# A transformer layer on one core: held and separate PSUM banks, 128-row gate sums, and casts issued behind bank copies

## The chip, the cores and the metric

One core of a Trainium2 chip runs the kernel. The metric is the device time in microseconds; the kernel before took 1955.86 us (median of 1954.67, 1955.86 and 1956.07). TensorE (PE) multiplies, VectorE (DVE) and ScalarE (ACT) do elementwise work, GpSimd (POOL) little, and SyncE (SP) issues DMAs.

## What is computed

One layer in f32, with T = 256 tokens, D = 2048 and DFF = 5632: two SwiGLU blocks with a token mixer between them, each modulated by columns of a vector `ada` and closed by a residual and a layer norm.

```python
ada = silu(c) @ w_ada + b_ada                   # 9 x 2048: shift, scale, gate of three blocks
h = swiglu(modulate(x, sh1, sc1), ffn1_w_in, ffn1_w_out)
x = layernorm(ALPHA * x + 0.5 * (1 + g1) * h, ln1_g, ln1_b)
z = modulate(x, sh2, sc2) @ w_in                # mixer
#   fox attention, 8 heads of 128: softmax(q k / sqrt(128) + F[q] - F[k], causal) v,
#     F = cumsum(log_sigmoid(forget gate))
#   mLSTM, 4 heads, 128 wide keys, 256 wide values: gates i and f, a running maximum,
#     rms norm, times sigmoid(o)
x = layernorm(ALPHA * x + (1 + g2) * (concat(fox, mlstm) @ w_out), ln2_g, ln2_b)
h = swiglu(modulate(x, sh3, sc3), ffn2_w_in, ffn2_w_out)
x = layernorm(ALPHA * x + 0.5 * (1 + g3) * h, ln3_g, ln3_b)
```

## The kernel before, in words

**Products.** Each f32 operand is split into a rounded part `hi` and the rest `lo` (both fp32r), and each product is three (`mm3`, L376 to L379: hi·hi, hi·lo, lo·hi). `load_w` (L359) brings a weight piece of 1 MB into one of three `raw` slots by an SP DMA, and `split` makes `hi` with an ACT cast (L145) and `lo` with a DVE subtraction (L146), in two or four parts, into six slots each. Products add up in PSUM banks of 512 f32 columns: five for `mm_tile`, three for `aux_tile`.

**Stages**, by the trace in us: start 0 to 40; first stage to 310; the rest of ffn1's input product (`ffn_in`) to 540; its output product (`out_proj`) to 770; a boundary with residual, layer norm, modulation and transposes to 840; the mixer to 1150, its output product to 1190; the second boundary to 1230; ffn2 to 1650 and 1938; the tail (`to_out`) to 1951.

**First stage** (`first_in`, L751). While the vector `ada` is still being made, the input product of ffn1 runs in four quarters j of the contraction, each with the same twelve units i of 48 products. A unit fills two banks; they are drained into SBUF (`hT`) at the end of each unit, by an ACT copy in quarter 0 and by DVE additions (L767) later. Last comes SiLU, 256 columns at a time. Beside it, `first_ada` makes the modulation columns of the next quarter: DMA'd rows `ar` are multiplied into an accumulator by DVE (L158 first, then L160; one named `gate` in even quarters). Of eight loads per quarter six sit in `raw` slots of the weights. Four pairs of column products (L718) and four small additions (L720) follow, between the four quarters of the modulated x (`xhi_f`, `xlo_f` L319). Later rows of `ada` go through `acc` (L160) throughout the kernel, a few pieces at a time ("pump", "step").

**out_proj** holds back its last weight pieces and does row block a = 0 of the last columns before a = 1 (`last_products`, L438). Where a boundary follows, a = 0's products are made as two passes of 256 columns; `add_up` (L447) multiplies the bank by the gate row (L453), adds the residual (L455) and takes the statistics (L457). The tail does so with both row blocks, scales (L613), shifts (L618) and stores (L619).

**Mixer.** `cols_form_b` and `form_a_pair` make the columns of w_in, ten groups: sigmoid inputs `mo` come ahead of them, then `fv` and `mv` (values), pairs `m` and `f` (queries and keys). Copies by ACT bring the banks to SBUF. Heads are generators in a list `side`, and a `step` after each half group takes a piece of one. A fox head (L985) puts into a bank q·k of two query blocks (128 and 256 keys wide, plain f32) and, for each, twice an 8-row product (L995) that adds the row −F (`nfrow`, hi and lo): a column of `rowsel` spread over 128 columns selects the head's row. An mLSTM head (L1103) does the same with 4-row products for `gb` (L1110). `gates` (L1044) makes those rows. The sigmoids `og` (L1173) read the `mo` banks; `ytp` (L1159) are transposes of mLSTM results; `bc` and L214 make a gate row of ada.

A scheduler of the tile framework orders each engine's instructions, by its own costs; `tc.manual_schedule` keeps an engine in program order, `tc.issue_after(x)` puts what is issued behind x, and an engine executes its list strictly in order. What a DMA or a semaphore wait stops on an engine stops all behind it.

## Time and profile before

| What | Value |
|---|---|
| Time, median of 3 | 1955.86 us (1954.67 to 1956.07) |
| The profiled execution | 1953.24 us, of which the trace spans 1951.1 |
| PE busy | 1898.5 us, 97% |
| DVE, ACT busy | 1461.1 us (75%), 939.9 us (48%) |
| Chain that ended last | PE 92%, DVE 5%, DMA 1% |
| Read from memory | 506.71 MB, 261 GB/s over the span |

A row of the timeline has its start, its duration, engine, line, operation, output tile and inputs, shapes and a count; a bracket holds idle time of the engine just before it and what ended that. A count over 1 groups rows of one form that follow each other, and the duration is then of all. Matmul rows overlap: what one costs PE is the distance from its start to the next one's, not its length. A plain f32 product appears as two records.

### The profile page before, as it was taken

What the parts mean: (1) busy time and instruction counts of PE and PEld (TensorE: products, weight loads), DVE (VectorE), ACT (ScalarE), POOL (GpSimd) and SP (SyncE); (2) the same over time, 40 slices, a digit from 0 to 9 for tenths busy, and PEclk for the clock granted to TensorE, in tenths of its full rate; (3) what the DMA queues carried; (4) which work ended last, traced back from release to release, by engine and by line L of the source; (5) the groups of instructions that cost most, each with busy time, mean ns of one, the idle gap of its engine ahead of it and who ended that gap; (6) DMA issues with size and microseconds to landing.
All of it is one profiled execution on the core that took longest, in us unless ns stands there. A gap on an engine that the chain in (4) does not pass through costs nothing.

```text
span 1951.1 us, 32572 instructions
## 1 busy us (share of the span) xinstructions
PE 1898.5 (97%) x13297; PEld 1741.2 (89%) x13297; DVE 1461.1 (75%) x1773; ACT 939.9 (48%) x1306; POOL 19.0 (1%) x34
## 2 busy tenths in 40 slices
PE   3999999999999999999999999999999999999997
PEld 3999999999988888598998886999999999988886
DVE  7889889777778898678877677767776654555776
ACT  2654454444444554645754544555444444444552
POOL 0000000000000000000000000000000000000000
PEclk9999999999999999999999999999999999999999
DMA  8999869999889887589878784997777755655552
GB/s 325 347 334 332 304 211 318 326 307 328 293 304 317 272 296 234 163 299 320 294 245 290 246 263 150 321 311 263 238 268 257 231 193 193 233 187 190 194 194 87
DMA packets 301821, 510.92 MB, mean 262 GB/s; under 512 B 10818, under 2 KB 158690, under 8 KB 300648
## 3 DMA queue, kind: packets, MB, share of 16 engines
q1 hardware_dynamic: 300808, 505.70, 76.5%
q0 software_dynamic: 864, 3.15, 0.5%
q8 instruction: 104, 1.70, 0.4%
q14 instruction: 45, 0.37, 0.1%
HBM read 506.71 MB, written 2.10 MB: 261 GB/s over the span
## 4 chain that ended last, share of the span: by engine, by line
PE 92%; DVE 5%; DMA 1%; issue 1%; ACT 1%; POOL 0%; DVEq 0%; SPq 0%; POOLq 0%; ACTq 0%
PE gu_f L379 8%; PE gu_f L377 8%; PE gu_f L378 8%; PE o_f L377 8%; PE o_f L379 8%; PE o_f L378 8%; PE s L377 5%; PE s L379 5%; PE s L378 5%; PE pr_f L378 2%; PE pr_f L377 2%; PE pr_f L379 2%; PE fh L377 2%; PE fh L378 1%; PE fh L379 1%; PE fs L378 1%
## 5 line engine op out<-in xcount | busy, mean ns | idle before, releaser
L160 DVE SCALAR_TENSOR_TENSOR acc<-ar,csil,acc 128x1024 f32<-128x1024 f32 x242 | 307.0, 1269 | 24.6 <-DMA ar<-in_w_ada_dram 23.8
L377 PE MATMUL s<-xhi_f,hi_s 128*128 128x256 f32 x768 | 213.5, 278 | 0.6 <-ACT hi_s L145 0.6
L378 PE MATMUL s<-xlo_f,hi_s 128*128 128x256 f32 x768 | 213.2, 278 | 0.0
L379 PE MATMUL s<-xhi_f,lo_s 128*128 128x256 f32 x768 | 212.9, 278 | 0.0
L379 PE MATMUL gu_f<-xhi_f,lo_f2i 128*128 128x256 f32 x768 | 212.0, 276 | 0.0
L378 PE MATMUL gu_f<-xlo_f,hi_f2i 128*128 128x256 f32 x768 | 212.0, 276 | 0.0
L377 PE MATMUL gu_f<-xhi_f,hi_f2i 128*128 128x256 f32 x768 | 212.0, 276 | 0.0
L146 DVE TENSOR_TENSOR lo_f2i<-raw_f2i,hi_f2i 128x1024 fp32r<-128x1024 f32 x96 | 117.6, 1225 | 99.9 <-ACT hi_f2i L145 99.8
L377 PE MATMUL gu_f<-xhi_f,hi_f1i 128*128 128x256 f32 x640 | 176.8, 276 | 0.0
L379 PE MATMUL gu_f<-xhi_f,lo_f1i 128*128 128x256 f32 x640 | 176.7, 276 | 0.0
L378 PE MATMUL gu_f<-xlo_f,hi_f1i 128*128 128x256 f32 x640 | 176.7, 276 | 0.0
L145 ACT CAST hi_f2i<-raw_f2i 128x1024 fp32r<-128x1024 f32 x96 | 100.8, 1050 | 137.5 <-PE gu_f L378 125.5
L145 ACT CAST hi_s<-raw_s 128x1024 fp32r<-128x1024 f32 x96 | 97.3, 1049 | 102.7 <-DMA raw_s<-in_ffn_w_in_dram 58.9
L377 PEld LDWEIGHTS s<-xhi_f,hi_s 128*128 128x128 f32 x768 | 145.2, 189 | 0.7 <-ACT hi_s L145 0.7
L145 ACT CAST hh<-hT 128x512 fp32r<-128x512 f32 x128 | 78.6, 621 | 138.6 <-PE o_f L378 136.9
L378 PEld LDWEIGHTS s<-xlo_f,hi_s 128*128 128x128 f32 x768 | 145.2, 189 | 0.0
L379 PEld LDWEIGHTS s<-xhi_f,lo_s 128*128 128x128 f32 x768 | 144.8, 189 | 0.3 <-DVE lo_s L146 0.3
L378 PEld LDWEIGHTS gu_f<-xlo_f,hi_f2i 128*128 128x128 f32 x768 | 144.2, 188 | 0.1
L377 PEld LDWEIGHTS gu_f<-xhi_f,hi_f2i 128*128 128x128 f32 x768 | 144.1, 188 | 0.1
L379 PEld LDWEIGHTS gu_f<-xhi_f,lo_f2i 128*128 128x128 f32 x768 | 144.2, 188 | 0.0
L146 DVE TENSOR_TENSOR lo_f2o<-raw_f2o,hi_f2o 128x1024 fp32r<-128x1024 f32 x88 | 107.7, 1224 | 44.9 <-ACT hi_f2o L145 44.8
L377 PE MATMUL o_f<-hi_f2o,hh 128*128 128x512 f32 (+1 forms) x368 | 139.4, 379 | 0.0
(451 smaller groups left out, 5357.6 us busy)
## 6 DMA issues: line engine op xcount, KB each, us to landing
ar<-in_w_ada_dram SPq DMA_DIRECT2D x288, 512.0 KB, 5.8
raw_s<-in_ffn_w_in_dram SPq DMA_DIRECT2D x48, 1024.0 KB, 5.9
raw_f2i<-in_ffn_w_in_dram SPq DMA_DIRECT2D x48, 1024.0 KB, 5.1
raw_f1o<-in_ffn_w_out_dram SPq DMA_DIRECT2D x44, 1024.0 KB, 7.2
raw_f2o<-in_ffn_w_out_dram SPq DMA_DIRECT2D x44, 1024.0 KB, 5.1
raw_f1i<-in_ffn_w_in_dram SPq DMA_DIRECT2D x40, 1024.0 KB, 7.8
raw_mxo<-in_w_out_dram SPq DMA_DIRECT2D x16, 1024.0 KB, 7.3
raw_fh<-in_ffn_w_in_dram SPq DMA_DIRECT2D x16, 1024.0 KB, 7.6
```

Of the source, the lines that this page charges most:

```text
L145: S.copy(hi, src)
L146: V.tensor_tensor(out=lo, in0=src, in1=hi.bitcast(F32), op=ALU.subtract)
L160: ins = V.scalar_tensor_tensor(out=acc, in0=raw, scalar=csil[:, k:k + 1], in1=acc, op0=ALU.mult, op1=ALU.add)
L377: PE.matmul(o, ah, bh, start=start, stop=False)
L378: PE.matmul(o, ah, bl, start=False, stop=False)
L379: return PE.matmul(o, al, bh, start=False, stop=stop)
```

## The change

1. *Ends by a bank of their own* (`last_products`, `add_up`): the last products of a row block run 512 wide up to the last four k; for those, columns 0 to 255 are finished in the old bank and columns 256 to 511 in a second bank `oh`. The first bank is multiplied by the gate row and added over all 512 columns, then `oh` is over its 256. In the tail both row blocks end so; at both boundaries too, where a = 1 was one pass of 512 columns. The tail's shifts and stores are put in another order, two pieces of 256 last for each row block.
2. *Held banks*: quarter j + 1 starts with the unit with which quarter j ended (`order_of`), so that unit goes on in the same two banks and is not drained between. SiLU is done 512 wide when both its parts are there. From the second quarter on, all eight column products go into one bank with one addition. The sums of the next quarter's `ada` are issued behind the last `xlo` of the current one (`behind`).
3. *128-row products*: −F's hi and lo stand in rows 0 to 7 and 32 to 39 of one tile `frows` of 128 rows, the rest zero, with the first 128 keys repeated, so that one product of 384 columns adds all of a fox head's rows; likewise `grows` for an mLSTM head.
4. *Casts behind bank copies*: in a group of the mixer, the splits of all weight pieces but the first are issued behind the last copy out of the previous group's banks (`emptied`). The sigmoids count as such copies, and a one-column sigmoid (`table`) is issued ahead to load the table.

```diff
     def load_w(src, nk, w, name, place=None, copies=()):
...
-            split(raw[:, q * h:(q + 1) * h, :], hi, lo)
+            with behind_copies(copies):
+                split(raw[:, q * h:(q + 1) * h, :], hi, lo)
...
+            def last_products(a):
+                half[a, 0] = mm_tile(f"oh_{tag}{a}")
+                args = held[:-kn] + (kept if a else []) + held[-kn:]
+                body, end = args[:-4], args[-4:]
+                with tc.issue_after(last[0].ins) if a else nullcontext():
+                    products(a, body, k0, None)
+                    products(a, end, None, ends[1], w=256)
+                    last.append(products(a, end, *ends, outs=half, c=256, w=256))
...
             def add_up(a, ps=ps, col=col, bs=range(nb), half=half):
...
+                    cs = slice(c0, c0 + 512)
+                    V.tensor_tensor(out=p, in0=p, in1=gate[:, cs], op=ALU.mult)
+                    V.scalar_tensor_tensor(out=r, in0=r, scalar=ALPHA, in1=p, op0=ALU.mult, op1=ALU.add)
+                    if half:
+                        p, cs = half[a, b][:, 256:], slice(c0 + 256, c0 + 512)
+                        V.tensor_tensor(out=p, in0=p, in1=gate[:, cs], op=ALU.mult)
+                        V.tensor_tensor(out=res[:, a, cs], in0=res[:, a, cs], in1=p, op=ALU.add)
...
     def to_out(products, add_up, st, lgb):
...
-                if a:
-                    second(0, 1536, 2048)
-                    second(1, 0, 256)
-                    second(1, 256, 512)
-                for j in range(a, 3 + a):
+                for j in range(3):
                     second(a, j * 512, (j + 1) * 512)
+                for j in range(2):
+                    second(a, 1536 + j * 256, 1792 + j * 256)
...
     def first_ada(j, ws=iter(())):
...
+            with behind(modulated[0]):
+                for h in range(2):
...
+        if j:
+            columns()
...
     def first_in(j, n, i, ws):
+        old = held.pop(i, None)
+        pss = old or [mm_tile(f"s{j}_{i}_{b}") for b in range(2)]
+        hold = n == NS - 1 and j < 3
+        if hold:
+            held[i] = pss
+            return
+    def order_of(j):
+        return [i % NS for i in range(NS - j, 2 * NS - j)]
...
     def fox_head(qs, h):
+        PE.matmul(lps[:, :3 * P], row_of(h), frows, start=True, stop=False)
         for qt in range(2):
-            PE.matmul(lps[:, cs], qs[:, 0, qt * P:(qt + 1) * P], qs[:, 1, :nk], start=True, stop=False)
-            for i in range(2):
-                PE.matmul(lps[:, cs], rowsel[:, h:h + 1].to_broadcast([8, P]), nfrow[i][:, :nk],
-                          start=False, stop=i == 1)
+            PE.matmul(lps[:, cs], qs[:, 0, qt * P:(qt + 1) * P], qs[:, 1, :P * (qt + 1)],
+                      start=False, stop=qt == 1)
...
-        for i in range(2):
-            PE.matmul(gb[:, :T], rowsel[:4, h:h + 1].to_broadcast([4, P]), ng[i], start=i == 0, stop=i == 1)
+        PE.matmul(gb[:, :T], row_of(h), grows, start=True, stop=True)
...
+    table = sm.tile([P, 1], F32, tag="table", bufs=1, name="table")
+    tc.keep_in_program_order(S.activation(table, ident[:, 0:1], AF.Sigmoid))
     for a in range(2):
         for h in range(NMH):
-            S.activation(og[h][:, a, :MV], mps[a, h // 2][:, h % 2 * MV:(h % 2 + 1) * MV], AF.Sigmoid)
+            sig = S.activation(og[h][:, a, :MV], mps[a, h // 2][:, h % 2 * MV:(h % 2 + 1) * MV], AF.Sigmoid)
+    emptied.append(sig)
```

On PE, where the pair group f0 ends, before (`ytp` are mLSTM transposes, `lps` a fox head's scores, `pr_f` the next group):

```order
L379 MATMUL pr_f_10672<-xhi_mx,lo_f0b_10923 128x256
L1159 MATMUL ytp_10958<-ident,og_8634 128x128 x4
L1159 MATMUL ytp_10969<-ident,og_8635 128x128 x4
L993 MATMUL lps_10980<-qs_10353 128x128
L995 MATMUL lps_10980<-nfrow_8644,rowsel 128x128
L995 MATMUL lps_10980<-nfrow_8645,rowsel 128x128
L993 MATMUL lps_10980<-qs_10353 128x256
L995 MATMUL lps_10980<-nfrow_8644,rowsel 128x256
L995 MATMUL lps_10980<-nfrow_8645,rowsel 128x256
L377 MATMUL pr_f_11024<-xhi_mx,hi_f1a_11028 128x256
```

The same place with the change (lines are those of the changed kernel):

```order
L390 MATMUL pr_f_10595<-xhi_mx,lo_f0b_10846 128x256
L1220 MATMUL ytp_10881<-ident,og_8554 128x128 x4
L1220 MATMUL ytp_10892<-ident,og_8555 128x128 x4
L1051 MATMUL lps_10903<-frows,rowsel 128x384
L1054 MATMUL lps_10903<-qs_10277 128x128
L1054 MATMUL lps_10903<-qs_10277 128x256
L388 MATMUL pr_f_10941<-xhi_mx,hi_f1a_10945 128x256
```

Four products of a head with 8 rows have become one with 128, ahead of the two of q and k.

On ACT, at the start of the mixer, before (`hi_fv` are casts of the value weights, `og` the sigmoids of the `mo` banks):

```order
L351 CAST xhi_mx<-xf_8427 128x2x128
L145 CAST hi_fv_00_8675<-raw_fv_0_8673 128x520
L145 CAST hi_fv_01_8691<-raw_fv_0_8673 128x520
L145 CAST hi_fv_02_8707<-raw_fv_0_8673 128x520
L145 CAST hi_fv_03_8723<-raw_fv_0_8673 128x520
L145 CAST hi_fv_10_8745<-raw_fv_1_8743 128x520
L1173 ACT_TABLE_LOAD
L1173 ACTIVATE og_8632<-mo_8436 128x256
L1173 ACTIVATE og_8633<-mo_8436 128x256
L1173 ACTIVATE og_8634<-mo_8437 128x256
L1173 ACTIVATE og_8635<-mo_8437 128x256
```

And with the change:

```order
L356 CAST xhi_mx<-xf_8347 128x2x128
L1233 ACT_TABLE_LOAD
L1233 ACTIVATE table<-ident 128x1
L145 CAST hi_fv_00_8599<-raw_fv_0_8597 128x520
L145 CAST hi_fv_01_8615<-raw_fv_0_8597 128x520
L145 CAST hi_fv_02_8631<-raw_fv_0_8597 128x520
L145 CAST hi_fv_03_8647<-raw_fv_0_8597 128x520
L1236 ACTIVATE og_8552<-mo_8356 128x256
L1236 ACTIVATE og_8553<-mo_8356 128x256
L1236 ACTIVATE og_8554<-mo_8357 128x256
```

The table load and a small sigmoid stand four casts ahead of the sigmoids, and the cast of fv's second weight piece (`hi_fv_10`) has moved behind them.

On DVE, at the end of the first quarter of the first stage, before (`lo_s` weights, `gate<-ar` the sums of ada, `scsh` the modulation columns, `xlo_f` the next quarter's x):

```order
L146 TENSOR_TENSOR lo_s_00_1068<-raw_s_0_1065,hi_s_00_1067 128x1024
L146 TENSOR_TENSOR lo_s_01_1072<-raw_s_0_1065,hi_s_01_1071 128x1024
L158 TENSOR_SCALAR gate<-ar_2_0_1075,csil 128x1024
L720 TENSOR_TENSOR scsh<-cp_987,bcol 128x2
L720 TENSOR_TENSOR scsh<-cq_988,bcol 128x2
L160 SCALAR_TENSOR_TENSOR gate<-ar_2_0_1075,csil,gate 128x1024
L720 TENSOR_TENSOR scsh<-cp_987,bcol 128x2
L720 TENSOR_TENSOR scsh<-cq_988,bcol 128x2
L319 TENSOR_TENSOR xlo_f_121<-xf_653,xhi_f_120 128x256 x4
L146 TENSOR_TENSOR lo_s_10_1135<-raw_s_1_1132,hi_s_10_1134 128x1024
L146 TENSOR_TENSOR lo_s_11_1139<-raw_s_1_1132,hi_s_11_1138 128x1024
L160 SCALAR_TENSOR_TENSOR gate<-ar_2_1_1142,csil,gate 128x1024 x2
```

And with the change:

```order
L146 TENSOR_TENSOR lo_s_110_1062<-raw_s_11_1059,hi_s_110_1061 128x1024
L146 TENSOR_TENSOR lo_s_111_1066<-raw_s_11_1059,hi_s_111_1065 128x1024
L739 TENSOR_TENSOR scsh<-cp_987,bcol 128x2x4
L324 TENSOR_TENSOR xlo_f_121<-xf_653,xhi_f_120 128x256 x4
L158 TENSOR_SCALAR gate<-ar_2_0_1069,csil 128x1024
L146 TENSOR_TENSOR lo_s_00_1127<-raw_s_0_1124,hi_s_00_1126 128x1024
L160 SCALAR_TENSOR_TENSOR gate<-ar_2_0_1069,csil,gate 128x1024
L146 TENSOR_TENSOR lo_s_01_1131<-raw_s_0_1124,hi_s_01_1130 128x1024
L160 SCALAR_TENSOR_TENSOR gate<-ar_2_1_1134,csil,gate 128x1024 x2
L146 TENSOR_TENSOR lo_s_10_1194<-raw_s_1_1191,hi_s_10_1193 128x1024
L146 TENSOR_TENSOR lo_s_11_1198<-raw_s_1_1191,hi_s_11_1197 128x1024
```

The four additions of columns are one, the four `xlo_f` come ahead of the sums, and a weight's `lo` stands between the sums of the first load.

More of the change, by code (lines that the diff above doesn't have):

```diff
@@ L438, in last_products @@
[L438 to L447 removed]
+                for k, hh, hl, hi, lo in args:
+                    for b in range(nb):
+                        bs = slice(b * 512 + c, b * 512 + c + w)
+                        mm = mm3(outs[a, b][:, c:c + w], hh[:, ts_], hl[:, ts_], hi[:, bs], lo[:, bs],
+                                 k == k0, k == k1)
@@ L712, in first_ada, with columns @@
             yield
-        cps = aux_tile(f"cp{j}"), mm_tile(f"cq{j}")
+        cps = aux_tile(f"cp{j}"), mm_tile(f"cq{j}") if j == 0 else None
+        def columns():
+            for q in range(4):
+                for v in range(2):
+                    PE.matmul(cps[0][:, 4 * v + q:4 * v + q + 1], acc[:, v, q * P:(q + 1) * P], ones[:, 0:1],
+                              start=True, stop=True)
+            js = slice(4 * j, 4 * j + 4)
+            V.tensor_tensor(out=scsh[:, 0:2, js], in0=cps[0][:, :8].rearrange("p (v k) -> p v k", v=2),
+                            in1=bcol[:, 0:2, js], op=ALU.add)
+        if j:
+            columns()
+            for _ in mb:
+                pass
+            yield
+            return
         def column(q):
@@ L978, in layer_kernel, with row_of @@
     fcol, mcol = ccol[:, :, 0:8], ccol[:, :, 8:12]
-    nfrow = [mx.tile([8, T], F32R, name=f"nfrow{i}") for i in range(2)]
-    rowsel = mx.tile([8, 8], F32R, name="rowsel")
-    V.tensor_copy(rowsel, ident[:8, :8])
+    frows = mx.tile([P, 3 * P], F32R, name="frows")
+    grows = mx.tile([P, T], F32R, name="grows")
+    lg2 = mx.tile([P, 2, 40], F32, name="lg2")
+    for t in (frows.bitcast(F32), grows.bitcast(F32), lg2):
+        G_.memset(t, 0.0)
+    rowsel = mx.tile([P, 8], F32R, name="rowsel")
+    V.tensor_tensor(out=rowsel, in0=ident[:, 0:8], in1=ident[:, 32:40], op=ALU.add)
+    def row_of(h):
+        return rowsel[:, h:h + 1].to_broadcast([P, P])
     def fox_head(qs, h):
```

141 lines of the change are left out of this document (73 added, 68 removed).

## The prediction

> **What bounds the kernel now.** I read the page's busy times first, then the table by stage, then PE's waits, then the timeline at each place that the diff touches.
>
> ```profile
> PE 1898.5 (97%) x13297; PEld 1741.2 (89%) x13297; DVE 1461.1 (75%) x1773; ACT 939.9 (48%) x1306; POOL 19.0 (1%) x34
> ```
>
> PE is busy for all but 53 us. By stage (PE, PEld, DVE, ACT and POOL busy, clock, DMA share, GB/s):
>
> ```profile
> 0.00:40.00 40.00, 7.49 (x32) 6.67 (x33) 29.09 (x43) 7.43 (x12) 2.37 (x11) 1.00 0.94 343
> 125.00:148.00 23.00, 23.00 (x205) 23.00 (x205) 22.19 (x24) 7.99 (x8) 0.00 (x0) 1.00 0.93 331
> 171.00:194.00 23.00, 23.00 (x202) 22.82 (x202) 22.78 (x31) 11.31 (x17) 0.73 (x1) 1.00 0.97 325
> 540.00:750.00 210.00, 210.00 (x944) 173.03 (x943) 179.89 (x194) 108.34 (x133) 0.53 (x1) 1.00 0.86 295
> ...
> 840.00:1150.00 310.00, 307.61 (x2135) 282.44 (x2135) 233.90 (x343) 174.25 (x297) 1.65 (x1) 1.00 0.83 281
> 1935.00:1952.00 17.00, 3.44 (x29) 3.24 (x27) 10.88 (x19) 0.00 (x0) 1.52 (x1) 0.69 0.34 123
> ```
>
> PE idles for 32.5 us at the start, which the change leaves alone, and for 13.6 us at the end, where DVE and the output's DMAs run; elsewhere for under 8 us. So what shortens PE's own stream in the mixer (840:1150) shortens the kernel, if loads keep up. The pace is 23/205 = 0.112 us for a 256-wide product and 210/944 = 0.222 for a mostly 512-wide one. In the first stage PE never stops, but DVE has only 0.8 and 0.2 of 23 us to spare in two of the stretches: that stage has nothing to give and something to lose. PE's waits between start and end are few; the two longest have their rows in parts 2 and 3, the next is that of the two boundaries (us in total, times, longest):
>
> ```profile
> PE tp L335 <- ACT n L331: 1.0, 2, 0.5
> ```
>
> **The change, part by part.** 1. *Rows of 128 in the mixer.* A fox head's scores, eight times in the program, and an mLSTM head's, four times:
>
> ```profile
> 1041.10 0.39 PE L993 MATMUL lps<-qs 128*128 128x128 f32 x2
> 1041.41 0.43 PE L995 MATMUL lps<-nfrow,rowsel 8*128 8x128 f32 x2
> 1041.78 0.70 PE L993 MATMUL lps<-qs 128*128 128x256 f32 x2
> 1042.40 0.50 PE L995 MATMUL lps<-nfrow,rowsel 8*128 8x256 f32 x2
> 1042.83 0.39 PE L377 MATMUL pr_f<-xhi_mx,hi_f1a 128*128 128x256 f32 x1
> 1043.05 0.28 PE L378 MATMUL pr_f<-xlo_mx,hi_f1a 128*128 128x256 f32 x1
> ...
> 952.93 0.28 PE L379 MATMUL pr_m<-xhi_mx,lo_m1b 128*128 128x256 f32 x1
> 953.14 0.50 PE L1110 MATMUL gb<-ng,rowsel 4*128 4x256 f32 x2
> 953.57 0.70 PE L1112 MATMUL sps<-o 128*128 128x256 f32 x2
> ```
>
> From start to start a fox head holds PE for 1042.83 − 1041.10 = 1.73 us, and the next product is 0.1 late: 1.83. The two kinds of product alternate. The 8-row ones take 0.37 + 0.43 = 0.80, the f32 ones 0.31 + 0.62 = 0.93, a change of kind included in each. Afterwards one 384-wide product of 128 rows, at 0.222 × 384/512 = 0.17, stands ahead of both f32 ones. With 0.93 for those the head takes 1.10 and saves 0.73; without the changes of kind between 128-row products (about 0.1 each, by the gap of 0.21 ahead of gb against 0.11) up to 1.0. I take 0.91: **−7.3** for eight (−5.8 to −8.0). For gb two products of 0.43 together become one of 0.11: 0.32, and 0.2 more if both changes of kind go; I take 0.32, **−1.3** for four (to −2.1). If 128 rows cost per column what 8 rows cost, half the columns go from lps (0.40) and half from gb (0.21): 8 × 0.50 + 4 × 0.21 = −4.9 in all, the small end.
>
> The Trainium skill, "TensorEngine Tiling (Array Packing)", section "Overview", speaks against this edit: a contraction of 32 rows or fewer leaves the array mostly unused and should be packed in tiles, up to four at once, not padded. No tiles run together here, and the rows show 0.2 us for 256 columns of 8 rows against 0.11 for 128 rows. Its section "Tiling Modes" says that a change of mode drains the engine; the 0.1 us ahead of gb agrees.
>
> 2. *Sigmoids (og) of the mixer.* The sigmoids' table load, and ahead of it a cast that waited 4.27 us for a slot, stand between the mo products and their banks:
>
> ```profile
> 836.64 0.63 ACT L145 CAST hi_fv<-raw_fv 128x520 fp32r<-128x520 f32 x1 [4.27 <-PE mo L379]
> 837.29 1.28 ACT L1173 ACT_TABLE_LOAD   x1
> 838.59 1.77 ACT L1173 ACTIVATE og<-mo 128x256 f32<-128x256 f32 x6
> 839.30 0.39 PE L377 MATMUL b_fv<-hi_fv,xhi_mx 128*128 128x264 f32 x1 [1.69 <-ACT og L1173]
> ```
>
> Afterwards the load goes four casts ahead and that cast behind the eight sigmoids. ACT idled 4.27 us, so 1.28 is covered there, and the first bank's sigmoids can run as its products end. PE gets back 1.69 + 0.2 around it: **−1.9** (0 if the sigmoids still come late). Behind the last sigmoid now wait the casts of fv's second load; the first load's four, split before, give PE 48 products, 5.4 us, meanwhile.
>
> 3. *A gate behind an ada sum.*
>
> ```profile
> 1025.09 0.40 PE L180 MATMUL bc<-alo,trir 128*128 128x512 f32 x1
> 1025.24 1.28 DVE L160 SCALAR_TENSOR_TENSOR acc<-ar,csil,acc 128x1024 f32<-128x1024 f32 x1 [3.59 <-DMA ar<-in_w_ada_dram]
> ...
> 1027.58 1.28 DVE L214 SCALAR_TENSOR_TENSOR gate<-bc,gate 128x512 f32<-128x512 f32 x2
> 1028.32 0.66 PE L1159 MATMUL ytp<-ident,og 128*128 128x128 f32 x4 [2.39 <-DVE gate L214]
> ```
>
> DVE stood for 3.59 us at a sum whose rows had not landed; the gate, and PE behind it, waited. In the new order that sum follows both gates. They can start when bc ends, at about 1025.5, so PE's wait goes: **−2.4** (0 if the lo now ahead is late instead). Next late is the sum itself, which nobody awaits.
>
> 4. *Casts behind bank copies.* From the second half of a group's weights on, a cast waits for the previous group's last copy; the rest of ACT's queue, DVE's lo and PE stand behind it.
>
> ```profile
> 1040.36 1.05 ACT L145 CAST hi_f1b<-raw_f1b 128x1024 fp32r<-128x1024 f32 x1 [1.81 <-PE pr_f L378]
> ...
> 1048.58 0.50 ACT L1003 ACTIVATE s<-s,nm 128x256 f32<-128x256 f32 x1
> 1050.04 1.20 ACT L1005 ACTIVATE s<-s,nm 128x256 f32<-128x256 f32 x3
> ```
>
> Half a group is 48 products, 5.4 us. The copies of a pair (two of at most 0.9, an estimate from the cast's 1.05 for twice the width) and the split (1.05, and on DVE half of the 2.36 that part 5 has for two) need about 4.0, which fits. In the first fox change (f0 to f1) the new order puts the cast behind a head's Exp (2.6 us, 1048.58 to 1051.2): I reckon it begun 6.3 us after the copies begin and split 2.3 later, 8.6, against PE's 8.3 (5.4 of products, two heads of 1.0, 0.9 of ytp), a stall of 0.3 to 1. **+1** for all ten groups (0 to +3).
>
> 5. *First stage.* Two drains per quarter less (1.28 together, the row at 120.14 below) is DVE time; PE was not waiting. One bank for the column sums saves a few changes of kind, **−0.4**. Against that, the ada sums now wait for the last xlo, and one of their loads sits in a weight slot:
>
> ```profile
> 103.18 1.28 DVE L160 SCALAR_TENSOR_TENSOR gate<-ar,csil,gate 128x1024 f32<-128x1024 f32 x1
> 105.92 0.76 DVE L319 TENSOR_TENSOR xlo_f<-xf,xhi_f 128x256 fp32r<-128x256 f32 x2 [0.63 <-ACT xhi_f L317]
> 112.84 2.36 DVE L146 TENSOR_TENSOR lo_s<-raw_s,hi_s 128x1024 fp32r<-128x1024 f32 x2 [0.79 <-ACT hi_s L145]
> ...
> 120.14 1.28 DVE L767 TENSOR_TENSOR hT<-hT,s 128x512 f32<-128x512 f32 x2
> ...
> 104.49 0.37 SPq L361 DMA_DIRECT2D raw_s<-in_ffn_w_in_dram  x1
> ```
>
> The load issued at 104.49 is released by the sum ending at 104.46. In the new order that sum follows all four xlo (done at 106.7), a first step and a lo, so it ends at 110 to 111 and the load starts 6 us later, at two of the quarter changes, with three more ada loads ahead of it on SP. That load's first half was split by 114.0, and PE began on it when the unit before ended, which the drain at 120.14 marks: 6.1 us of slack against 6 to 7 of delay, a stall of about 1 each: **+2** (0 to +6; the upper end if DVE, with 0.2 to 0.8 us to spare, cannot catch up).
>
> 6. *Ends of the products.* Tail (and the same form at both boundaries):
>
> ```profile
> 1938.48 0.43 DVE L453 TENSOR_TENSOR o_f<-o_f,gate 128x256 f32<-128x256 f32 x1 [1.24 <-PE o_f L379]
> ...
> 1940.32 0.69 DVE L457 BATCH_NORM_STATS2 st_f<-res 128x6 f32<-128x512 f32 x1
> ...
> 1943.81 3.52 DVE L618 SCALAR_TENSOR_TENSOR res<-res,rs_last,lb 128x512 f32<-128x512 f32 x6
> ```
>
> All four operations up to the statistics (1938.48 to 1940.32) waited for PE's end; now two do, as the other 256 columns' bank ends 12 products (1.35 us) earlier and its 512-wide pair (about 1.4) runs meanwhile: −0.8. One 512-wide last step moves ahead into row block 0: −0.6. Together **−1.4** (−0.7 to −1.9). At the two boundaries row block 0 gains 0.9 but row block 1, which was added up in two operations, now has four; DVE runs back to back from there, and PE waits for it again (the 1.0 at tp): **0** (−1.8 to +1.8). In the mixer's output the end of row block 0 reaches the last unit early, and its lo is not ready:
>
> ```profile
> 1181.72 0.28 PE L377 MATMUL o_mx<-hi_mxo,yhi 128*128 128x256 f32 x1
> ...
> 1182.22 0.28 PE L379 MATMUL o_mx<-hi_mxo,ylo 128*128 128x256 f32 x1
> ...
> 1182.70 0.28 PE L377 MATMUL o_mx<-hi_mxo,yhi 128*128 128x256 f32 x1
> ...
> 1183.36 0.28 PE L379 MATMUL o_mx<-hi_mxo,ylo 128*128 128x256 f32 x1
> ```
>
> Twice two products take 0.50 and 0.66 instead of 0.23. Afterwards the 512-wide passes over the older units come first, and the lo is there: **−0.7** (0 to −0.7).
>
> Sum: −7.3 − 1.3 − 1.9 − 2.4 + 1 − 0.4 + 2 − 1.4 − 0.7 = **−12.4 us**. The profiled execution took 1953.24 (span 1951.1), 2.6 under the median of 1955.86; so the median becomes 1955.86 − 12.4 = **1943.5**. About 0.2%, 3.9 us, is what a measurement of this kernel can tell from no change.
>
> **The rivals.** *A, slower: each cast behind a copy holds PE.* If all ten groups' casts land behind a head's Exp operations (1048.58 to 1051.2, 2.6 us) with 0.8 of slack, that is +18 in place of +1: 1960.5. It decides from 1.35 us per group (no gain left), 1.75 for slower by 0.2%. For it: one group is that late in the new order. Against: the others aren't.
>
> *B, the mixer is fed, not computed.* If its loads (0.83 DMA share) set the pace, the shorter heads only make PE wait for lo: 8.6 lost, 1952. For it: the sum at 1025.24 waits for DMA. Against: the cast at 1040.36 waits for PE to free its slot.
>
> *C, 128 rows cost per column what 8 rows cost* (−4.9 for −8.6): 1947. For it: no row here has a broadcast weight with 128 rows. Against: every other 128-row product runs at 0.11. [...]
>
> *D, first stage late:* +8 in place of +2. The three ada loads ahead of the late weight are 0.52 MB each (128x1024 f32), 1.6 us at the table's 331 GB/s; if the weight waits for all three, each change stalls for about 4 us rather than 1: 1949.5. For it: DVE at 22.78 of 23. Against: the drains give DVE 1.3 us back per quarter.
>
> **How the numbers follow.** Forecast 0.55 (own range 1938 to 1948), C 0.14, D 0.13, B 0.10, A 0.08. The range must leave out no more than 0.2: 1937 to 1953 leaves out A and the edges. Faster by over 0.2% (below 1951.9): forecast, C, nearly all of D and a third of B, 0.83. Within: the rest of B and a little of A and D, 0.10. Slower: 0.07.
>
> **What would show it.** Right: 0.8 to 1.0 between lps and the next pr_f; no wait of b_fv on og nor of ytp on gate; a last DVE run that ends 1.4 us nearer to PE's end. Wrong: new PE waits on lo_s around 120 and 186 us (D), on lo of f, m or fv in the mixer (A, B), a frows product above 0.3 us (C). More than 5 us of any of these breaks the forecast.

## The result, and the profile after

The changed kernel takes **1944.89 us** (median of 4, 1943.69 to 1946.44) against 1955.26 for the kernel before (1953.64 to 1956.07): a ratio of 0.9948, with a 95% interval of 0.9931 to 0.9966. That is 10.4 us less, where 12.4 were forecast. The two profiled executions differ by less, 6.8 us (1953.24 and 1946.44; spans 1951.1 and 1944.7), because the profiled one of the changed kernel was the longest of its four and that of before lies 2.0 under its median. What follows is read from these two profiles, so it has to explain 6.4 us of span.

The busy times of the page after:

```profile
PE 1893.7 (97%) x13197; PEld 1737.9 (89%) x13197; DVE 1458.4 (75%) x1753; ACT 931.4 (48%) x1294; POOL 19.4 (1%) x37
```

PE is busy for 4.8 us less than before, DVE for 2.7. PE's waits after (us in total, times, longest); the three long ones at the start of the program are as before and left out:

```profile
PE s L388 <- ACT hi_s L145: 1.8, 2, 1.2
PE tp L340 <- DVE n L334: 1.3, 1, 1.3
PE s L390 <- DVE lo_s L146: 1.1, 2, 0.8
...
PE ytp L1220 <- DVE gate L214: 0.6, 1, 0.6
```

The wait of `b_fv` on `og` is gone and that of `ytp` on `gate` fell from 2.4 to 0.6. New are waits in the first stage (`s` waited 0.6 in all before, 2.9 now) and one of 1.3 at a boundary (`tp`, 0.4 at most before on the same `n`). So the change took waits out of the mixer and brought others elsewhere. Where, is read from the first start of each stage's products (by the timeline) in both traces; the last column is what the stretch since the row above gained or lost:

| First PE start of | before | after | stretch |
|---|---|---|---|
| `gu_f`, end of the first stage | 311.82 | 316.31 | +4.5 |
| `b_fv`, start of the mixer's groups | 837.09 | 840.34 | −1.2 |
| `b_mv`, second group | 862.15 | 863.38 | −2.0 |
| `ytp`, end of the first fox pair | 1025.32 | 1027.25 | +0.7 |
| `lps`, first fox head | 1041.10 | 1041.34 | −1.7 |
| `ge`, ffn2's first product | 1200.60 | 1195.62 | −5.2 |
| `fh`, after the second boundary | 1231.33 | 1227.14 | +0.8 |
| PE's last product | 1938.16 | 1933.33 | −0.6 |
| end of the span | 1951.09 | 1944.71 | −1.5 |

The heads. A fox head after, from `lps` to the next group's products, and an mLSTM head's `gb` with its neighbours:

```profile
954.99 0.28 PE L390 MATMUL pr_m<-xhi_mx,lo_m1b 128*128 128x256 f32 x1
955.11 0.28 PE L1171 MATMUL gb<-grows,rowsel 128*128 128x256 f32 x1
955.23 0.59 PE L1173 MATMUL sps<-o 128*128 128x256 f32 x2
...
1041.34 0.42 PE L1051 MATMUL lps<-frows,rowsel 128*128 128x384 f32 x1
1041.60 0.82 PE L1054 MATMUL lps<-qs 128*128 128x128 f32 x4
1042.07 0.47 PE L388 MATMUL pr_f<-xhi_mx,hi_f1a 128*128 128x256 f32 x1
1042.37 0.28 PE L389 MATMUL pr_f<-xlo_mx,hi_f1a 128*128 128x256 f32 x1
```

A head now holds PE for 1042.07 − 1041.34 = 0.73 us, and the product behind it is 0.30 instead of 0.11 from the next one, so 0.19 late: 0.92, against 1.84 before. `gb` costs 0.12, like any product of 256 columns, and nothing waits in front of it: from the product ahead to `sps` 0.24 instead of 0.64.

The start of the mixer, ACT and PE:

```profile
838.48 2.72 ACT L1236 ACTIVATE og<-mo 128x256 f32<-128x256 f32 x8 [2.97 <-PE mo L390]
840.58 0.28 PE L390 MATMUL b_fv<-hi_fv,xlo_mx 128*128 128x256 f32 x1
840.69 0.29 PE L388 MATMUL b_fv<-hi_fv,xhi_mx 128*128 128x264 f32 x1
```

The sigmoids start when their bank is done (ACT stood 2.97 us ready), and PE goes from product to product 0.11 apart. The gate ahead of `ytp`:

```profile
1026.57 1.22 DVE L146 TENSOR_TENSOR lo_f1a<-raw_f1a,hi_f1a 128x1024 fp32r<-128x1024 f32 x1 [0.85 <-ACT hi_f1a L145]
1027.71 1.28 DVE L214 SCALAR_TENSOR_TENSOR gate<-bc,gate 128x512 f32<-128x512 f32 x2
1028.45 0.66 PE L1220 MATMUL ytp<-ident,og 128*128 128x128 f32 x4 [0.60 <-DVE gate L214]
```

The sum that waited for its DMA no longer stands here. A `lo` that waits for its cast does, and leaves 0.60.

The first stage. DVE's queue after the first quarter, and SP's:

```profile
107.20 0.76 DVE L324 TENSOR_TENSOR xlo_f<-xf,xhi_f 128x256 fp32r<-128x256 f32 x2 [0.76 <-ACT xhi_f L322]
107.88 0.75 DVE L158 TENSOR_SCALAR gate<-ar,csil 128x1024 f32<-128x1024 f32 x1
108.54 1.22 DVE L146 TENSOR_TENSOR lo_s<-raw_s,hi_s 128x1024 fp32r<-128x1024 f32 x1
109.68 1.28 DVE L160 SCALAR_TENSOR_TENSOR gate<-ar,csil,gate 128x1024 f32<-128x1024 f32 x1
...
102.42 1.63 SPq L709 DMA_DIRECT2D ar<-in_w_ada_dram  x3
110.98 1.50 SPq L371 DMA_DIRECT2D raw_s<-in_ffn_w_in_dram  x2
```

The weight that was issued at 104.49 is issued at 110.98, 6.5 us later, behind the sum that ends at 110.96. PE did not stop there. It stopped later, in the second half of the second and of the third quarter:

```profile
160.10 0.39 PE L390 MATMUL s<-xhi_f,lo_s 128*128 128x256 f32 x1 [0.32 <-DVE lo_s L146]
...
229.38 0.38 PE L388 MATMUL s<-xhi_f,hi_s 128*128 128x256 f32 x1 [1.18 <-ACT hi_s L145]
...
230.64 0.58 PE L390 MATMUL s<-xhi_f,lo_s 128*128 128x256 f32 x1 [0.76 <-DVE lo_s L146]
```

The stretches around that place, by the table of windows (PE, PEld, DVE, ACT and POOL busy, clock, DMA share, GB/s; the clock is what PE was granted, as a share of full speed):

```profile
171.00:194.00 23.00, 23.00 (x205) 23.00 (x204) 19.32 (x24) 10.85 (x17) 0.73 (x1) 1.00 0.83 285
217.00:240.00 23.00, 21.06 (x169) 20.66 (x168) 20.40 (x24) 9.61 (x10) 0.00 (x0) 0.93 0.91 305
...
227.17:230.58 3.41, 1.53 (x12) 1.13 (x10) 1.22 (x2) 1.99 (x2) 0.00 (x0) 1.00 1.01 364
230.58:233.99 3.41, 3.35 (x15) 3.35 (x16) 3.41 (x6) 2.40 (x3) 0.00 (x0) 0.50 0.82 266
234.00:237.41 3.41, 3.41 (x31) 3.41 (x31) 3.41 (x5) 2.04 (x3) 0.00 (x0) 1.00 0.93 300
```

The three waits are 0.32 + 1.18 + 0.76 = 2.3 us. In the 3.41 us up to 230.58 PE stood for 1.88; in the next 3.41 it was granted half the clock and started 15 products, and then 31 again: about 1.7 us lost on top of the waits. A stretch of 23 us that holds 205 products elsewhere holds 169 here. At 171 to 194 DVE is less busy than before (19.32 against 22.78). The two drains of one unit, 1.28 us, are gone there, and DVE waits more for casts; that did not make up for the late weights.

The second boundary: the last bank of row block 0 and DVE's work on it (PE, then DVE), and PE's next stop:

```profile
1181.89 0.28 PE L390 MATMUL oh_mx<-hi_mxo,ylo 128*128 128x256 f32 x1
...
1182.88 0.68 DVE L466 TENSOR_TENSOR o_mx<-o_mx,gate 128x512 f32<-128x512 f32 x1
1183.59 0.69 DVE L468 SCALAR_TENSOR_TENSOR res<-res,o_mx 128x512 f32<-128x512 f32 x1
1184.20 0.43 DVE L472 TENSOR_TENSOR oh_mx<-oh_mx,gate 128x256 f32<-128x256 f32 x1
...
1185.11 0.69 DVE L476 BATCH_NORM_STATS2 st_mx<-res 128x6 f32<-128x512 f32 x1
...
1194.63 0.66 PE L340 MATMUL tp<-ident,n 128*128 128x128 f32 x4 [1.30 <-DVE n L334]
```

And the tail, DVE:

```profile
1933.82 0.42 DVE L472 TENSOR_TENSOR oh_f<-oh_f,gate 128x256 f32<-128x256 f32 x1
1934.73 0.69 DVE L476 BATCH_NORM_STATS2 st_f<-res 128x6 f32<-128x512 f32 x1
1938.22 2.86 DVE L637 SCALAR_TENSOR_TENSOR res<-res,rs_last,lb 128x512 f32<-128x512 f32 x5
```

In the tail two operations of 256 columns now lie between PE's end and the statistics, and the run ends 1941.08 − 1933.82 = 7.26 us after it began, against 1947.33 − 1938.48 = 8.85.

### The profile page after: what moved, and what is told of

Same layout as the page of the kernel before. It is cut to its first block, busy times and chain, and to the rows that moved or that the text cites. A ratio compares the mean times of both kernels' runs of the same rounds, so it can differ in the third digit from the quotient of the medians.

```text
span 1944.7 us, 32312 instructions
## 1 busy us (share of the span) xinstructions
PE 1893.7 (97%) x13197; PEld 1737.9 (89%) x13197; DVE 1458.4 (75%) x1753; ACT 931.4 (48%) x1294; POOL 19.4 (1%) x37
## 4 chain that ended last, share of the span: by engine, by line
PE 72%; issue 11%; DVE 9%; DMA 5%; ACT 2%; POOL 0%; SPq 0%; DVEq 0%; ACTq 0%; POOLq 0%
PE gu_f L389 8%; PE gu_f L388 8%; PE gu_f L390 8%; PE o_f L388 8%; PE o_f L390 8%; PE o_f L389 8%; PE s L388 3%; PE s L390 3%; PE s L389 2%; DMA raw_s<-in_ffn_w_in_dram 2%; DMA raw_mxo<-in_w_out_dram 2%; DVE gate L160 2%; PE fh L388 2%; PE fh L389 1%; PE fh L390 1%
## 5 line engine op out<-in xcount | busy, mean ns | idle before, releaser
L146 DVE TENSOR_TENSOR lo_s<-raw_s,hi_s 128x1024 fp32r<-128x1024 f32 x96 | 114.4, 1220 | 38.0 <-ACT hi_s L145 37.7
```

Of the source, the lines that this page charges most:

```text
L146: V.tensor_tensor(out=lo, in0=src, in1=hi.bitcast(F32), op=ALU.subtract)
```

## The experiments

**The first stage.** *a*: the changed kernel with the ada sums free again.

```diff
     def behind(ins):
-        return tc.issue_after(ins.ins) if ins else nullcontext()
+        return nullcontext()
```

> The changed kernel, but the sums of the next quarter's ada are no longer issued behind the last xlo; all else as changed. Theory (a weight slot is held by the waiting sum): the third weight load of the second quarter is issued near 104.5 us again instead of 111.0, PE's waits on hi_s and lo_s (2.9 us in the changed kernel's profile) go, the first stage ends 4 us earlier, and the time is about 1941 us, 0.7% under the kernel before. Rival (the held banks or the one bank for the columns make the first stage longer): the first stage still ends near 316 us and the time stays at 1945.

Measured: 1940.22 us, ratio 0.992 [0.9907, 0.9933], 4.7 under the changed kernel (5.5 by the ratios). The weight is issued early again and the stretch that had 169 products has 205:

```profile
102.55 0.37 SPq L372 DMA_DIRECT2D raw_s<-in_ffn_w_in_dram  x1
```

```profile
217.00:240.00 23.00, 23.00 (x205) 23.00 (x204) 19.17 (x24) 10.20 (x10) 0.00 (x0) 1.00 0.92 333
```

So the order of the sums costs about 5 us in the changed kernel. The first stage ends at 311.02 here, 0.8 ahead of the kernel before; *e*, *i* and *j* below, with the same first stage, end it at 311.40 to 312.91, so what the held banks and the one bank for the columns gave is not to be seen. *l* does that part alone on the kernel before.

```diff
+    def behind(ins):
+        return tc.issue_after(ins.ins) if ins else nullcontext()
...
-            V.tensor_tensor(out=lo, in0=xf[:, q, :], in1=hi.bitcast(F32), op=ALU.subtract)
+            modulated[0] = V.tensor_tensor(out=lo, in0=xf[:, q, :], in1=hi.bitcast(F32), op=ALU.subtract)
...
+            with behind(modulated[0]):
```

> The kernel before with the ada sums behind the last xlo alone. Theory (the sum that waits holds a weight slot): the weight load after the first quarter's end is issued 5 to 6.5 us later than 104.5, PE waits on hi_s and lo_s in the second and third quarters by 2 to 5 us in all, and the time is 2 to 5 us above the kernel before. Rival (only together with the rotated units does the order hurt): the same time within 0.5 us.

Measured: 1962.14 us (1955.17 to 1965.61), 1.0035 [1.0023, 1.0046], 7 us slower than before, more than the 2 to 5 expected. SP issues the weight at 109.34, and PE waits:

```profile
PE s L384 <- DVE lo_s L146: 1.5, 3, 0.8
```

So this order is a loss without the rest of the change too. The profiled execution is the shortest of these runs, and only 2 us of its first stage show it; the longer runs have a mean granted clock of 0.995 to 0.997 against 0.998 in *a*. A stretch of 3.41 us at half clock, like the one at 230.58 above, costs 1.7 us and takes 0.0009 off that mean (half of 3.41 over 1953). This profile has one, at 1130.93, and a mean of 0.997; 0.995 would be one or two more (an estimate, no trace of a long run exists). The rest of the 7 us is not explained. *h* takes the held banks out of *a*:

```diff
-        hold = n == NS - 1 and j < 3
+        hold = False
...
-            if j == (1 if i == NS - 1 else 0):
+            if j == 0:
...
-        return [i % NS for i in range(NS - j, 2 * NS - j)]
+        return list(range(NS))
```

> The changed kernel with the sums free (as in a_sums_free), without the held banks: each quarter of the first stage takes the units in the order 0 to 11 and drains all twelve. Theory (the two drains are DVE's time, for which PE does not wait once the sums are free): the same as a_sums_free within 0.5 us, 1940.2. Rival (the slack of the weights is so small that 1.3 us of DVE's time per quarter are seen): 1 to 3 us slower, with waits of PE on lo_s in the second and third quarters.

Measured: 1942.16 us (1939.57 to 1951.14), 0.9931 [0.9916, 0.9946]. The interval overlaps that of *a*, so this run does not decide what held banks are worth. Its profiled execution is the longest of its runs by 7.9 us: `s` waits 2.8 us for `xhi_f` and 2.2 for `xlo_f`, which *a* does not have, and a stretch at half clock follows at 184.30.

**The 128-row products.** *b*: that part alone on the kernel before, with the rows laid out as in the change.

```diff
+        PE.matmul(lps[:, :3 * P], row_of(h), frows, start=True, stop=False)
...
-            for i in range(2):
-                PE.matmul(lps[:, cs], rowsel[:, h:h + 1].to_broadcast([8, P]), nfrow[i][:, :nk],
-                          start=False, stop=i == 1)
...
-        for i in range(2):
-            PE.matmul(gb[:, :T], rowsel[:4, h:h + 1].to_broadcast([4, P]), ng[i], start=i == 0, stop=i == 1)
+        PE.matmul(gb[:, :T], row_of(h), grows, start=True, stop=True)
```

> The kernel before with the 128-row products of frows and grows alone. Theory (each head's saving is PE's, 0.92 us for a fox head by the two profiles, about 0.4 for an mLSTM head): 8 x 0.92 + 4 x 0.4 = 9 us, about 1946. Rival 1 (what heads save is given back in the mixer's other products, which in the changed kernel's profile stand 0.122 us apart instead of 0.118): 5 us, about 1950. Rival 2 (the mixer waits for its loads): 2 us or less, above 1953, with waits of pr_f on lo.

Measured: 1947.35 us, 0.9956 [0.9944, 0.9967]: −8.1 where −8.6 was forecast for heads and `gb`. Its profile has a stretch at half clock at 1025.74, behind the wait of `ytp`. The other two waits of the mixer stay, as they should:

```profile
PE ytp L1166 <- DVE gate L214: 2.6, 1, 2.6
PE b_fv L377 <- ACT og L1180: 1.7, 1, 1.7
```

**The casts.** *c*: the changed kernel with casts free of the copies.

```diff
     def behind_copies(copies):
-        return tc.issue_after(copies[-1].ins) if copies else nullcontext()
+        return nullcontext()
```

> The changed kernel without the casts behind bank copies; the table load stays ahead. Theory (the order behind copies matters at the first fv group alone, where a cast stands ahead of the sigmoids again): a wait of PE on og of about 0.5 us, all else within 0.5; the time about 1945 to 1946. Rival 1 (they hold PE at other groups): faster, 1942 to 1943. Rival 2 (they are what keeps copies early throughout the mixer): 3 us or more slower, 1948.

Measured: 1950.52 us, 0.9972 [0.9958, 0.9987]: 5.6 *slower* than the changed kernel. In its profile 1.5 us of that stand already at the end of the first stage (317.77), which the edit does not touch (a stretch at half clock lies there, at 162.69), so the order that was forecast to cost 1 us is worth some 4. More than half stands on DVE ahead of `ytp`:

```profile
1029.72 1.28 DVE L160 SCALAR_TENSOR_TENSOR acc<-ar,csil,acc 128x1024 f32<-128x1024 f32 x1 [4.73 <-DMA ar<-in_w_ada_dram]
1030.92 1.22 DVE L146 TENSOR_TENSOR lo_f1a<-raw_f1a,hi_f1a 128x1024 fp32r<-128x1024 f32 x1
1032.05 1.28 DVE L214 SCALAR_TENSOR_TENSOR gate<-bc,gate 128x512 f32<-128x512 f32 x2
```

The sum that waits for its rows is back ahead of the gate, and PE waits 3.0 us for it, not 0.6. Right behind that wait, at 1033.09, lies a second stretch at half clock, 1.7 us more. So the gate's place, forecast as an effect of its own, follows from the casts' order. *g* does the casts (and the early table load) alone on the kernel before; `emptied` is filled as in the change, and the small sigmoid is written into an existing tile.

```diff
-            split(raw[:, q * h:(q + 1) * h, :], hi, lo)
+            with behind_copies(copies):
+                split(raw[:, q * h:(q + 1) * h, :], hi, lo)
...
+    table = em[:, 0, 0:1]
+    tc.keep_in_program_order(S.activation(table, ident[:, 0:1], AF.Sigmoid))
```

> The kernel before with the casts behind bank copies and the early table load alone (the small sigmoid writes into em, so no address moves). Theory (both of PE's waits, that on og and that on the gate, go by the order that these casts make; nothing else changes): 1.9 + 1.8 = 3.7 us less, about 1951.7. Rival (they hold PE at the other groups, as the prediction priced them): 1 us less of that, about 1953. Rival (they gain beyond these two waits): below 1950.

Measured: 1951.99 us, 0.9986 [0.9976, 0.9996], 2.0 under the median of before beside it and 2.7 by the ratio. `b_fv` no longer waits; two other waits stand:

```profile
PE ytp L1169 <- DVE gate L214: 1.8, 1, 1.8
PE o_mx L384 <- DVE lo_mxo L146: 0.8, 2, 0.7
```

So of the expectation the sum came out and the parts did not: the gate's wait went from 2.4 to 1.8, not to nothing. By the stage starts of this run, from `b_fv` to `b_mv` it gained 2.0 and from `ytp` to `lps` 1.1, and from `lps` to `ge` it lost 2.2: 0.6 is the longer wait of `o_mx`, and 1.7 a stretch at half clock at 1097.70. The same edit is worth some 4 in the one kernel and some 2.4 in the other; in both a stretch at half clock is in the sum, and it need not come in every run.

**The ends.** *d*: the changed kernel with the `last_products`, `add_up`, boundary and tail of before.

```diff
-                half[a, 0] = mm_tile(f"oh_{tag}{a}")
...
+                if a == 0:
+                    last.append(products(a, held, w))
+                    return
...
-            products(0)
-            products(1)
+            products(0, 256)
+            products(1, 256)
```

> The changed kernel with the ends of the output products, the sums behind them and the tail's stores as before (two passes of 256 columns, one bank). Theory: the tail gets 1.5 us longer, the mixer's output 0.2 to 0.7, the boundaries together 0.4; the time about 1947. Rival (the boundaries' a = 1, with four operations for two, costs what the rest brings): the same time within 0.5 us, 1945.

Measured: 1952.81 us (1948.08 to 1957.28, 12 runs), 0.9982 [0.9973, 0.9992], where about 1947 was expected. The profiled execution, near the lowest, is 2.7 us over the changed kernel's: by the stage starts, the tail is 1.6 longer, the end of ffn2 0.6, the stretch with the first boundary 0.4, the second boundary 0.8 shorter, and `ytp` to `lps` 0.7 longer, since `ytp` waits 1.3 for the gate and not 0.6. So the ends themselves are 1.8 here. The median is 7.9 over the changed kernel's. The runs up to 1950.84 have a mean granted clock of 0.998, the longer ones 0.995 to 0.997, which would be one to three stretches at half clock (an estimate by the 0.0009 for each); the profiled execution has none. Where they lie, and whether the old ends have a part in it, no trace shows; the ends are worth 1.8 by the profiles and more by the medians, and why is left open.

**An address.** The products of the mixer's groups take longer after: 380 steps of `pr_m` from start to start are 46.2 us instead of 45.4. Between the two kernels some of the later tiles of SBUF, the mixer's x among them, moved by 32 bytes per partition, because of the 4-byte tile `table`; x went from byte 139104 to 139136 of its partition, 96 and 128 beyond a multiple of 256. *f* adds such a tile, and nothing else, to the kernel before:

```diff
+    pad = sm.tile([P, 1], F32, tag="pad", bufs=1, name="pad")
+    G_.memset(pad, 0.0)
```

> The kernel before with an unused one-column tile in the pool sm (one memset by GpSimd), which moves the mixer's x by 32 bytes and nothing else. Theory of the moved address: pr_m and pr_f slower by about 2 to 3 ns a product, 2 to 4 us in all, about 1958 against 1955.5. Rival (the pace has another cause): the same time, pr_m at 45.45 us.

Measured: 1958.23 us, 1.002 [1.0011, 1.003], 4 us slower. Its profile has three stretches at half clock, so runs of one granted clock say more: at 0.998, three of this kernel took 1955.97 to 1958.02 and ten of the kernel before beside them 1951.14 to 1953.00. *e* takes the shift out of *a*:

```diff
-    table = sm.tile([P, 1], F32, tag="table", bufs=1, name="table")
+    table = em[:, 0, 0:1]
```

> The changed kernel with the sums free (as in a_sums_free), and with the one-column sigmoid that loads the table written into an existing tile (em) instead of a tile of its own in the pool sm; that tile of 4 bytes moved everything allocated behind it, the mixer's x (xhi_mx, xlo_mx) among them, by 32 bytes per partition. Theory (products read their moving operand slower at the moved address: pr_m's products are 119.5 to 122 ns apart in all four kernels that have the tile, 117 to 118 in the one without): the products pr_m take 44.7 us between their starts instead of 46.16, pr_f 1 to 2 us less, the whole about 3 us less than 1940.2: 1937. Rival (the pace is slower because casts and copies run beside the products at other times): pr_m stays at 46.16 and the time at 1940.

Measured: 1938.69 us, 0.9918 [0.9903, 0.9933]. The products are faster again, as below, by 2.4 us over `pr_m` and `pr_f`, but the total is only 1.5 under *a* with overlapping intervals, where 3 was expected. PE waits 0.4 for a `lo` of f0 instead, and the gate's wait is back:

```profile
PE ytp L1221 <- DVE gate L214: 3.1, 1, 3.1
```

In *a* it is 0.6. The `lo` that stands ahead of the gate waits for a cast, which in *a* waits 3.73 us for its weight's DMA and starts at 1020.09; here the cast starts at 1021.70. So the order alone does not fix what the gate gained. *i*, *j* and *k* put x elsewhere with a tile of 128, 64 and 128 bytes: at 224 in *e*, at 160 in *e*, at 224 in the kernel before. The edit (16 in place of 32 for *j*):

```diff
+    pad = sm.tile([P, 32], F32, tag="pad", bufs=1, name="pad")
+    G_.memset(pad, 0.0)
```

> As e_sums_free_no_shift, with an unused tile of 128 bytes per partition in the pool sm, so that the mixer's x starts at byte 224 of 256 in its partition, as ffn's x does (whose products are 113.3 ns apart), instead of byte 96 (118 to 121) or, with the 32 bytes of the change, 128 (120 to 122). Theory (the pace follows from where the moving operand starts within 256 bytes): pr_m 43.2 us instead of 44.7, pr_f 3 to 4 us less, the whole 4 to 5 us less, about 1934. Rival (ffn's pace has another cause): pr_m at 44.7 or above, the time 1938 to 1939.

> As e_sums_free_no_shift, with an unused tile of 64 bytes: x starts at byte 160 of 256, 32 of 64 as at 96 and 224. Theory A (what counts is the start within 64 bytes): pr_m at 44.7 as at byte 96, or at 43.2 as at 224 if those two differ for another reason; the time 1934 to 1939. Theory B (it counts within 256): pr_m anywhere between 43.2 and 46.2.

> The kernel before with the unused tile of 128 bytes alone (one memset by GpSimd). Theory of the start within 256 bytes: pr_m 43.2 to 43.5 us instead of 45.45, pr_f 3 us less, the whole 4 to 5 us less than the kernel before. Rival: the same time as before, or slower by 2 to 4 us as with the 32 bytes (any move of the addresses costs).

Measured: *i* 1936.92 us, 0.9912 [0.9899, 0.9925]; *j* 1937.99, 0.9917 [0.9905, 0.9929]; *k* 1951.78, 0.9987 [0.9977, 0.9997]. The first 32 products of one kind of `pr_m` (ns of one: least, median, most; first and last start), in the kernel before, the changed one and *i*:

```profile
L377 PE MATMUL pr_m<-xhi_mx,hi_m0a x32: 278/280/280, 910.9 to 922.0; 128*128 128x256 f32 x32
```

```profile
L388 PE MATMUL pr_m<-xhi_mx,hi_m0a x32: 277/280/289, 912.3 to 923.5; 128*128 128x256 f32 x32
```

```profile
L389 PE MATMUL pr_m<-xhi_mx,hi_m0a x32: 276/276/283, 908.7 to 919.3; 128*128 128x256 f32 x32
```

From the first to the last of these starts lie 93 products: 11.1, 11.2 and 10.6 us. Over the 380 steps of `pr_m` it is 43.5 us with x at 224 (*i*, *k*), 44.7 (*b*, *e*) and 45.4 (before, *g*, *l*) at 96, 45.2 at 160 (*j*), and 46.2 at 128 (the changed kernel, *a*, *c*, *d*, *f*, *h*). The kernels of one place differ widely in the order of ACT and DVE, and at 224 and at 128 their sums are equal to 0.02 us, so the place sets the pace there. At 96 there are two values, 44.7 with the 128-row products and 45.4 without them, and why is open. Of the two expectations for *j*, that only the place within 64 bytes counts, falls: 96, 160 and 224 are alike in it, and *e*, *j* and *i*, which differ in the place alone, have 44.7, 45.2 and 43.5.

*i* has the lowest median of this study, 8.0 us under the changed kernel and 17 under the one before; its interval overlaps those of *e* and *j*. The gain over *e* is 1.8, where 4 to 5 was expected: `ytp` waits 3.2 us for the gate here too. *k* gained 2.7 by its ratio where 4 to 5 was expected; its profile has two stretches at half clock, at 839.26 and 1026.99, behind the waits on `og` and on the gate.

## Why the prediction was right

The sign, the time (1943.5 for 1944.9) and the main terms, heads, `og` and tail, were right. That the median came within 1.4 us is in part luck: the first stage cost 2.9 more than forecast and a shift that was not in the sum 2.4 to 2.9, so that by the two profiles the forecast is 6.0 us too good. Point by point, in the profiles:

- **Heads (−8.6): right.** Measured −0.92 per fox head (forecast −0.91) and −0.40 per `gb` (−0.32). *b* alone gave 8.1. Rival C falls: a product of 128 rows and 384 columns holds PE for 0.26 us with the change of kind behind it. For contractions of 32 rows or fewer, the Trainium skill, "TensorEngine Tiling (Array Packing)", "Overview", offers independent tiles, with up to four times the speed in theory. That was not tried, and no other product ran beside these; padding to 128 rows paid (*b*).
- **og (−1.9): right**, −2.0. **Gate (−2.4): sized a little high**, −1.8, because the step "they can start when bc ends" failed: a `lo` that waits for its cast stands in that place. And the step "in the new order that sum follows both gates" is right only while the casts stand behind the copies (*c*). The −1.8 is not secure either: in *e*, *i* and *j*, of the same order, the wait is 3.1, 3.2 and 1.7.
- **Casts (+1): wrong in sign**, since the changed kernel is slower without them (*c*) and the kernel before faster with them (*g*, the gain of `og` in it). The step that failed is that a cast set behind a copy only holds PE back. In the first fox change the cast came 4.8 us after the copies began, not 6.3, and its `lo` was there within 0.1 of PE. Rival A had no weight at all, and rival B neither, as a mechanism: only 0.3 us at the last head's transposes and 0.2 at the first `ylo` of the output product are waits of that kind. What was overlooked is that the same order moves the gate ahead of the sum, so its price and the gate's gain are one term.
- **First stage (+1.6): mechanism right, too small**, +4.5. The load was issued late by the 6 us forecast, but no "stall of about 1 each" came at the quarter changes, where the weight was still ready 2.1 us ahead of PE. The lateness was not made up in the quarter that followed; it met PE in its second half. The half clock after it, 1.7 us, was not in the sum. That is between the forecast and rival D (+8), which has the right place but waits for three loads.
- **Boundaries (0): −1.2 and +1.7.** The second lost 0.9 at `tp` and 0.8 up to `fh`. The step "row block 0 gains 0.9" failed there: its first bank was ready early, but DVE was still adding up the columns ahead and came to it at 1182.88, so from its last product to its statistics it took 1185.11 − 1181.89 = 3.2 us, against 2.2 before (1187.94 to 1190.11 in that trace). Stretch −1.2 holds the rest of ffn1 with the first boundary. With the old ends (*d*) it is −0.8, so 0.4 of it comes from the ends; where the rest comes from was not tried.
- **Mixer's output (−0.7): −0.5**, since the gaps went and one wait of 0.2 came. **Tail (−1.4): right**, −1.55.
- **Not in the sum:** the shift of x, +2.9 on `pr_m` and `pr_f` (+0.7 and +2.2, from start to start; *a* and *e*, which differ in the shift alone, are 2.4 apart), and −0.6 at ffn2's end, where fewer products are 256 wide.

Over the mixer these add up. From `b_mv` to `ge` PE's time by output tile, from start to next start, went from 14.17 to 5.88 for `lps`, 4.41 to 2.74 for `gb` and `sps`, 4.29 to 2.41 for `ytp`, 46.10 to 46.77 for `pr_m`, 91.32 to 93.56 for `pr_f`, 2.09 to 2.72 for the heads' transposes, 22.47 to 22.93 for the second `fv` group and 90.62 to 92.19 for the output product with its wait at `tp`: −6.3 in all, and the stage starts say −6.2.

In the profiles the forecast is 6.0 us too good, and most of it is the first stage (2.9) and the shift (2.4 to 2.9); the other misses nearly cancel. By the medians it is 2.0, because the profiled execution of the changed kernel was a long one and that of before a short one. The stretch at half clock has a part in that: the profile of before has none, and two of the changed kernel's four runs (1943.69 and 1945.20) have a mean granted clock of 0.998 where the profiled one has 0.997. No trace of those two exists.

## What to carry to other kernels

A product that adds a few rows by selection is cheaper as one of full height than as several thin ones, if its operand can be laid out with zeros: a thin product of 256 columns held PE for 0.2 us and a full one for 0.12, and changes of kind cost some 0.1 each. Before an order is put behind another, follow the DMA that the moved work releases to the end of the *next* period and not only to the next use, since an engine with little slack carries lateness forward. And when stage times move that the change does not touch, compare the pace of single products: a new small tile may have shifted an operand.

## What the runs showed of the hardware

*The place of the moving operand.* Products of 256 columns take 114 to 122 ns (43.5 to 46.2 us for 380) in kernels that differ in where x begins in its partition: 96, 128, 160 or 224 bytes beyond a multiple of 256. At 224 it is least, at 128 most, and a 4-byte tile cost 4 us in *f*. Only these four places were tried, other tiles moved along with x, and that 256 bytes is the period is not shown.

*The clock.* In the 14 traces, from 50 us to PE's last products, the granted clock is 1.00 but for twelve stretches of 3.41 us at 0.50: one each in the changed kernel, *b*, *g*, *h* and *l*, two in *c* and *k*, three in *f*, none in the kernel before, *a*, *d*, *e*, *i* and *j*. Within a trace they lie whole multiples of 3.413 us apart (*c*: 162.69 and 1033.09, 255 of them). In the 3.41 us ahead of eight of them PE stood for 1.76 to 3.03 us; where it stood for 1.59 to 1.79 in such a stretch, in six other places, none followed. So PE standing for about half of a stretch was enough, in one wait (2.6 us in *b*) or in two close together (1.18 and 0.76). The other four, in *f*, *g* and *l*, follow two fox heads of the old form that fill 3.1 to 3.4 us of the stretch before, while PE has no idle time in it. The first of the two in *f*:

```profile
1100.75:1104.16 3.41, 3.41 (x17) 2.12 (x15) 1.86 (x5) 3.19 (x7) 0.00 (x0) 1.00 1.04 398
1104.16:1107.57 3.41, 3.41 (x9) 2.69 (x9) 3.26 (x11) 2.44 (x9) 0.00 (x0) 0.50 0.87 356
```

In *k* such a pair fills 3.38 us and nothing follows. Two heads of the new form fill at most 1.5 us of a stretch, and none of them is followed by half clock. That the thin products are the reason was not tried.

These stretches go with the spread between runs of one kernel: of the 64 runs of the kernel before that were taken beside the experiments, those with a mean granted clock of 0.998 have a median of 1952.59 us, those with 0.997 one of 1954.45 and those with 0.996 one of 1956.15. That is about the 1.7 us of one stretch for each 0.001.

The Trainium skill, "TensorE: Matmul & The Clock Gate", "Part 1: The HAM clock gate", halves the clock after an idle window of about 3.4 us. The length agrees with the 3.41 us here, but no wait was as long as that, and the clock fell all the same: the measurement decides, and two short waits close together are to be feared too. That page gives a busy window of the same length before full pace comes back; the 3.41 us from 230.58 to 233.99 agree.
